# Mixer B of a two-layer decoder trunk: group weights made in token rows and sent through scratch memory

## The chip, the cores and the metric

The kernel runs on one core of one Trainium2 chip. The metric is the device time of one execution in microseconds, as the median of several runs; lower is better. The trace is that of one profiled execution, and its times count from the start of its span.

## The reference

A trunk of two layers over 1024 tokens of width 1024, all in float32. Layer 1 is causal attention with a forget gate and a gated convolutional feed-forward network. Layer 2 begins with mixer B, which the change is in: three groups g = 0, 1, 2 of 8 heads each (head width 64), group g attending over tokens that lie 1, 4 or 16 apart. Every group gives, for each token and head, an output o_g and the logarithm of its softmax denominator, and the three are merged:

```
m = jnp.max(s, axis=-1, keepdims=True)
p = jnp.exp(s - m)
l = jnp.sum(p, axis=-1, keepdims=True)
o = einsum("bnrhij,bnjrhd->bnirhd", p / l, vv)
lse = (m + jnp.log(l))[..., 0]
...
alpha = jax.nn.softmax(jnp.stack(lses, axis=0), axis=0)
o = jnp.sum(alpha[..., None] * jnp.stack(outs, axis=0), axis=0)
x = x + o.reshape(B, S, B_OUT_WIDTH) @ b_w_out[bl]
```

After it come a second feed-forward network and a last norm.

## The kernel before

Activations lie with the features on the 128 partitions and the tokens along the free axis. Every float32 product of the projections is made as three matmuls of split halves (`mm3`, L114 to L116, 512 columns each).

Mixer B runs over 12 units (p, g): p counts four pairs of heads (j = 0, 1), and for each p the groups come in the order 2, 1, 0. `attend_b` (L488) works on one unit in two halves m of the tokens. `scores_b` (L459) makes the scores of one block of 128 queries (L475, L476) with the block's tokens on the partitions; for g = 1 and 2 the order of tokens is by residue, so that a block holds tokens that lie 4 or 16 apart. `softmax` (L251) adds the bias and takes the negative maximum `nm` on VectorE (L254), the exponential and its sum `ls` on ScalarE (L259), the reciprocal of the sum on VectorE (L261), and multiplies the probabilities by it on GpSimd (L262). `transposed_pv` turns the probabilities (L232, `tp`), splits them into `pt` (L150 on ScalarE, L151 on VectorE), and multiplies with the values into `po` (L245). `add_parts` adds the two halves of `po` into the group's output `og` (a ScalarE copy into `otmp`, L267, and a VectorE addition, L268).

When all three groups of a pair are there, `each_half` (L1281) takes the logarithm of all sums (L1273), subtracts the maxima (L1274), and calls `merge_b` (L520) for each half of 512 tokens. `merge_b` copies the statistics so that each value stands 64 times side by side (`lx`, L535), and turns them with TensorE so that each token's value lies on the 64 partitions of its head: four transposes for g = 0 (L539), four for g = 1 (L541), and eight matmuls against parts of the identity for g = 2 (L544; the trace counts two instructions for each, so 16 per half). Then maxima, differences, exponentials, sums, reciprocals and weighted additions run over tiles of 128x512 on VectorE, ScalarE and GpSimd (L548 to L564). The result is split by `emit_o` (L570) and written to scratch memory `o_sp` (for the last pair: kept in `yh`, `yl`).

Beside the attention, `weave` takes instructions from a filler: the projections of the unit ahead (`tasks_b`, L1217; their weights come by `load_half`, L82: one DMA on SyncE's queue into `wraw`, a gain on GpSimd at L89, a cast into `wh` at L92, a difference into `wl` at L93). In the last unit (3, 0) the filler is the first half of the output projection (`out_proj`, L600), which starts when the first token half of the last pair is merged. Earlier results come back from `o_sp` and the residual from `x_sp` at the start of that unit (`reload`, L582). The order of the instructions on each engine is set when the kernel is built, by a scheduler that simulates the engines and moves instructions against the order of the program; on the chip each engine and each DMA-issuing queue runs its list in that order.

Of the kernel before, what the change touches and what calls it, by code (L numbers as in the profile page):

```python
# [8 lines left out]
F32 = mybir.dt.float32  # L9
# [41 lines left out]
def trunk(ctx, tc, x, a_w_in, a_b_f, a_w_out, b_w_q, b_w_out, kv_norm_g, w_kv,  # L51
# [23 lines left out]
    aug = dram.tile([A_HEADS, 2, 4, S], F32, name="aug")  # L75

# [174 lines left out]
    def softmax(t, sc_cuts, masks, nm, l, rl):  # L251

        for ci, ((sc, a, b), m) in enumerate(zip(sc_cuts, masks)):
            nc.vector.tensor_tensor_reduce(  # L254
                out=t[:, a:b], in0=sc, in1=m, scale=1.0,
                scalar=INIT if ci == 0 else nm[ci - 1], op0=ALU.add, op1=ALU.min,
                accum_out=nm[ci])
# [3 lines left out]
        nc.vector.reciprocal(rl, l)  # L261
        nc.gpsimd.tensor_scalar(out=t[:, :n], in0=t[:, :n], scalar1=rl, scalar2=1.0,  # L262
                                op0=ALU.mult, op1=ALU.mult)

    def add_parts(dst, po, tmp, view=lambda t: t):

        nc.scalar.copy(tmp, po[64:P])  # L267
        nc.vector.tensor_tensor(out=dst, in0=view(po[0:64]), in1=view(tmp), op=ALU.add)  # L268
# [95 lines left out]
    def attend_a(ap, ps_, u, heads, v, last):  # L364
        psc, ptr, pov = ps_

        def values(qg, j, probs, o):
# [10 lines left out]
            tmp = ap.tile([P, 2 * P], F32, name="otmp", bufs=1)  # L378
            add_parts(o[js], po[:, :2 * P], tmp[js])
# [79 lines left out]
    def scores_b(ap, psc, p, g, j, head, nm, ls, m):  # L459
# [6 lines left out]
        rl = ap.tile([P, 4], F32, name="rl", bufs=2)  # L466
        cell = {}
        for b in range(4 * m, 4 * m + 4):
# [12 lines left out]
                    [nm[:, g, j, b:b + 1]], ls[:, g, j, b:b + 1],  # L481
                    rl[:, b - 4 * m:b - 4 * m + 1])
# [5 lines left out]
    def attend_b(ap, ps_, p, g, heads, v, og, nm, ls, each_half):  # L488
        psc, ptr, pov = ps_

        def values(m, j, cell):
# [14 lines left out]
            tmp = ap.tile([P, H2], F32, name="otmp", bufs=1)  # L506
            add_parts(in_order(g, og[js], m), po, tmp[js], residues(g))
# [4 lines left out]
        for m in range(2):  # L512
            for j in range(2):
                cell = yield from scores_b(ap, psc, p, g, j, heads[j], nm, ls, m)
# [5 lines left out]
    def merge_b(ap, psc, ls, os, hf):  # L520

        sl = half(hf)
        lt = []
        for g in range(NG):

            tp = psc.tile([P, H2], F32, name="sc")
            tpr = tp.rearrange("p (t r) -> p r t", r=DILS[g])
            blocks = [4 * hf + i for i in range(4)] if g == 0 else (
                [2 * i + hf for i in range(4)] if g == 1 else list(range(NB)))
            for i, b in enumerate(blocks):  # L530
                if i % 4 == 0:
                    lx = ap.tile([P, 4, 2, 64], F32, name="lx", bufs=2)
                    step = 2 if g == 1 else 1
                    src = ls[:, g, :, b:b + 4 * step - step + 1:step]
                    nc.scalar.copy(lx, src.rearrange("p j b -> p b j").unsqueeze(3)  # L535
                                   .to_broadcast([P, 4, 2, 64]))
                lb = lx[:, i % 4].rearrange("p j d -> p (j d)")
                if g == 0:
                    nc.tensor.transpose(tp[:, i * P:(i + 1) * P], lb, ident)  # L539
                elif g == 1:  # L540
                    nc.tensor.transpose(tpr[:, i], lb, ident)  # L541
                else:
                    own = ident.rearrange("p (r t) -> p r t", r=2)[:, :, 32 * hf:32 * hf + 32]
                    nc.tensor.matmul(tpr[:, 2 * b:2 * b + 2], lb, own, start=True, stop=True)  # L544
            lt.append(tp)
        mx = ap.tile([P, 4, 2, 64], F32, name="lx", bufs=2).rearrange("p b j d -> p (b j d)")
        e = [ap.tile([P, H2], F32, name=f"e{g}") for g in range(NG)]
        nc.scalar.copy(mx, lt[0])  # L548
        for g in (1, 2):
            nc.vector.tensor_tensor(out=mx, in0=lt[g], in1=mx, op=ALU.max)  # L550
        for g in range(NG):
            nc.vector.tensor_tensor(out=e[g], in0=lt[g], in1=mx, op=ALU.subtract)
            nc.scalar.activation(e[g], e[g], AF.Exp)
        nc.gpsimd.tensor_tensor(out=mx, in0=e[0], in1=e[1], op=ALU.add)
        nc.gpsimd.tensor_tensor(out=mx, in0=mx, in1=e[2], op=ALU.add)
        for i in range(4):
            c = slice(i * P, (i + 1) * P)
            nc.vector.reciprocal(mx[:, c], mx[:, c])  # L558
        for g in range(NG):
            eng = nc.gpsimd if g < 2 else nc.vector  # L560
            eng.tensor_tensor(out=e[g], in0=os[g][:, sl], in1=e[g], op=ALU.mult)
        nc.vector.tensor_tensor(out=e[1], in0=e[1], in1=e[2], op=ALU.add)
        nc.vector.tensor_tensor(out=e[0], in0=e[0], in1=e[1], op=ALU.add)
        nc.vector.tensor_tensor(out=e[0], in0=e[0], in1=mx, op=ALU.mult)  # L564
        return e[0]
# [624 lines left out]
    with ExitStack() as st:  # L1190
# [71 lines left out]

        filler = stream([t for i in range(len(units)) for t in tasks_b(i)])
# [70 lines left out]
```

## Time and profile before

| | us |
|---|---|
| median of 3 runs (2672.45 to 2673.91) | 2672.62 |
| the profiled execution | 2673.07 |
| its span, first to last instruction | 2671.2 |
| mixer B after its first projections, up to its last unit | about 1380 to 1880 |
| mixer B's last unit, up to the first matmul of the output projection | 1880 to 1919 |
| output projection, both halves | 1919 to 1965 |

In the views, PE is TensorE's matmuls, PEld its weight loads, DVE VectorE, ACT ScalarE, POOL GpSimd, SP SyncE. "Busy" is the time in which an engine had an instruction running; matmuls overlap, so the mean duration of one is longer than the time by which the next follows it. In a row of groups the numbers behind the bar are busy us, mean ns of one, and the idle time of the engine just before them with what ended it.

### The profile page before, as it was taken

How to read it: one execution, taken by the hardware profiler on the slowest of the kernel's cores; microseconds unless marked ns; L12 is line 12 of the kernel's file. 1: busy time of each engine (PE TensorE's matmuls, PEld its weight loads, DVE VectorE, ACT ScalarE, POOL GpSimd, SP SyncE). 2: the span in 40 equal slices, each digit the busy share in tenths (PEclk: the TensorE clock that was granted, in tenths of full speed). 3: DMA queues.
4: the chain of work that ended last, by engine and by line, in shares of the span. 5: the costliest groups of instructions: out<-in, count | busy, mean ns of one | idle time of the engine just before them, and what ended most of it. 6: DMA issues, size and time to landing. Idle time of an engine off the chain costs nothing.

```text
span 2671.2 us, 37824 instructions
## 1 busy us (share of the span) xinstructions
PE 2590.0 (97%) x12913; PEld 2165.8 (81%) x12913; DVE 2000.6 (75%) x4037; ACT 1378.6 (52%) x2893; POOL 658.0 (25%) x841
## 2 busy tenths in 40 slices
PE   7999999999999999999899999999889999999998
PEld 5898888787788888888688888888667888888887
DVE  6676777777877777778867777777798677776787
ACT  6566666654534444444545656665645434444444
POOL 0222322310122112112223453534301111111121
PEclk8999999999999999999999999999899999999999
DMA  5121211522111111111411111112321111111113
GB/s 183 51 64 50 57 50 56 195 87 91 44 52 49 54 52 58 53 52 47 145 36 36 45 43 40 41 36 76 115 91 48 48 56 48 53 59 56 48 48 114
DMA packets 251241, 175.40 MB, mean 66 GB/s; under 512 B 12448, under 2 KB 231208, under 8 KB 251048
## 3 DMA queue, kind: packets, MB, share of 16 engines
q1 hardware_dynamic: 250936, 172.96, 21.3%
q8 instruction: 102, 1.67, 0.3%
q14 instruction: 91, 0.75, 0.1%
q10 hardware_dynamic: 112, 0.02, 0.0%
HBM read 145.06 MB, written 23.68 MB: 63 GB/s over the span
## 4 chain that ended last, share of the span: by engine, by line
PE 85%; DVE 8%; ACT 3%; issue 2%; DMA 2%; POOL 0%; POOLq 0%; SPq 0%; ACTq 0%; DVEq 0%
PE up L754 30%; PE mm L114 13%; PE mm L115 13%; PE mm L116 13%; PE po L245 4%; PE tp L232 3%; PE sc L353 1%; DVE u L705 1%; PE sc L354 1%; DVE lx L558 1%; PE up L114 1%; DVE t L254 1%; PE sc L476 1%; PE sc L475 1%; PE up L115 1%
## 5 line engine op out<-in xcount | busy, mean ns | idle before, releaser
L114 PE MATMUL mm<-yh,wh 128*128 128x512 f32 x960 | 381.3, 398 | 12.2 <-ACT yh L150 5.9
L115 PE MATMUL mm<-yl,wh 128*128 128x512 f32 x960 | 379.5, 395 | 1.2 <-DMA yl<-o_sp 1.2
L116 PE MATMUL mm<-yh,wl 128*128 128x512 f32 x960 | 379.6, 395 | 0.0
L150 ACT CAST wh<-wraw 128x512 fp32r<-128x512 f32 x228 | 140.9, 619 | 353.8 <-PE up L754 306.7
L859 DVE TENSOR_TENSOR xT<-mm,xT 128x512 f32<-128x512 f32 x320 | 217.9, 684 | 108.8 <-PE mm L116 107.0
L151 DVE TENSOR_TENSOR wl<-wraw,wh 128x512 fp32r<-128x512 f32 x228 | 165.9, 733 | 152.1 <-ACT wh L150 152.0
L754 PE MATMUL up<-yh,wh 128*128 128x512 f32 x704 | 274.4, 390 | 0.9 <-ACT wh L150 0.9
L754 PE MATMUL up<-yl,wh 128*128 128x512 f32 x704 | 274.1, 389 | 0.0
L754 PE MATMUL up<-yh,wl 128*128 128x512 f32 x704 | 268.9, 389 | 0.0
L259 ACT ACTIVATE t<-t,nm 128x128 f32<-128x128 f32 (+4 forms) x320 | 185.2, 580 | 86.2 <-DVE nm L254 84.0
L115 PE MATMUL mm<-ml,wh 128*128 128x512 f32 x576 | 225.3, 391 | 1.4 <-DVE ml L151 1.4
L114 PE MATMUL mm<-mh,wh 128*128 128x512 f32 x576 | 224.8, 390 | 0.0
L116 PE MATMUL mm<-mh,wl 128*128 128x512 f32 x576 | 223.9, 389 | 0.0
L114 PEld LDWEIGHTS mm<-yh,wh 128*128 128x128 f32 x960 | 181.1, 189 | 49.8 <-ACT yh L150 6.2
L116 PEld LDWEIGHTS mm<-yh,wl 128*128 128x128 f32 x960 | 181.0, 188 | 34.3
L115 PEld LDWEIGHTS mm<-yl,wh 128*128 128x128 f32 x960 | 181.3, 189 | 33.8 <-DMA yl<-o_sp 1.4
L738 POOL TENSOR_TENSOR sraw<-fraw 128x512 f32<-128x512 f32 x40 | 67.1, 1677 | 547.3 <-DMA fraw<-in_ffn_w_up_dram 385.6
L150 ACT CAST pt<-tp 128x128 fp32r<-128x128 f32 (+2 forms) x408 | 148.6, 381 | 96.3 <-PE tp L232 55.2
L151 DVE TENSOR_TENSOR pt<-tp,pt 128x128 fp32r<-128x128 f32 (+2 forms) x408 | 168.7, 430 | 34.5 <-ACT pt L150 32.1
L245 PE MATMUL po<-pt,v 128*128 128x256 f32 x1040 | 190.0, 292 | 2.4 <-ACT pt L150 1.0
L245 PEld LDWEIGHTS po<-pt,v 128*128 128x128 f32 x1040 | 154.5, 191 | 17.3 <-DVE pt L151 1.5
L93 DVE TENSOR_TENSOR wl<-wraw,wh 128x512 fp32r<-128x512 f32 x176 | 129.4, 738 | 50.7 <-ACT wh L92 43.0
(350 smaller groups left out, 6307.6 us busy)
## 6 DMA issues: line engine op xcount, KB each, us to landing
wraw<-in_ffn_w_down_dram SPq DMA_DIRECT2D x104, 256.0 KB
fraw<-in_ffn_w_up_dram SPq DMA_DIRECT2D x88, 256.0 KB
wraw<-in_ffn_w_up_dram SPq DMA_DIRECT2D x88, 256.0 KB
wraw<-in_a_w_in_dram SPq DMA_DIRECT2D x60, 256.0 KB
wraw<-in_w_kv_dram SPq DMA_DIRECT2D x48, 256.0 KB
wraw<-in_a_w_out_dram SPq DMA_DIRECT2D x32, 256.0 KB
xT<-x_sp SPq DMA_DIRECT2D x32, 256.0 KB
wraw<-in_b_w_q_dram SPq DMA_DIRECT2D x24, 256.0 KB
```

The costliest lines, as they stand in the source:

```text
L93: nc.vector.tensor_tensor(out=wl, in0=raw, in1=wh.bitcast(F32), op=ALU.subtract)
L114: nc.tensor.matmul(ps, ah, bh, start=(i == 0), stop=False)
L115: nc.tensor.matmul(ps, ah, bl, start=False, stop=False)
L116: nc.tensor.matmul(ps, al, bh, start=False, stop=(i == n - 1))
L150: nc.scalar.copy(h, src)
L151: return nc.vector.tensor_tensor(out=l, in0=src, in1=h.bitcast(F32), op=ALU.subtract).ins
L232: nc.tensor.transpose(tp[:, i * P:(i + 1) * P], c, ident)
L245: nc.tensor.matmul(po[:, col:col + 2 * P], v(kb), pt[:, hl, i * 2 * P:(i + 1) * 2 * P], start=(first and i == 0 and hl == 0), stop=(last a ...
L259: nc.scalar.activation(t[:, :n], t[:, :n], AF.Exp, bias=nm[len(sc_cuts) - 1], scale=-1.0, accum_out=l)
L738: nc.gpsimd.tensor_tensor(out=raw[n], in0=raw[a], in1=raw[b], op=op)
L754: nc.tensor.matmul(ps[bank], a[:, c], b[:, k], start=(start and k == 0 and i == 0), stop=(k == KH - 1 and i == 2), skip_group_check=True)
L859: nc.vector.tensor_tensor(out=xT[:, d, sl], in0=ps, in1=xT[:, d, sl], op=ALU.add)
```

## The change

Probabilities stay unnormalised in mixer B: `softmax` gets no `rl` there, and its reciprocal (L261) and GpSimd multiplication (L262) are left out (layer 1 keeps them). The negative maxima and the sums of a pair are kept in one tile `st`, 32 columns for each group. When a unit is done, `spread` turns its 32 columns with one transpose into 32 rows of 128 tokens, copies them to SBUF, and writes them to scratch memory in the order of the tokens. `group_weights` reads them back for one token half as rows of 32 tokens on 32 partitions, makes the three weights exp(max difference) / (weighted sum) there, writes them to scratch, and reads them repeated on 64 partitions for each head. `merge_b` then is three multiplications and two additions. For the first three pairs, the weights are made in the middle of the next pair's first unit and the merge runs at its end; for the last pair both follow at once, half by half. `add_parts` writes the ScalarE copy straight to its destination and adds onto it, without `otmp`.

```
-        nc.vector.reciprocal(rl, l)
-        nc.gpsimd.tensor_scalar(out=t[:, :n], in0=t[:, :n], scalar1=rl, ...)
+        if rl is not None:   # the same two, for layer 1 alone
...
+    def add_parts(dst, po):
+        nc.scalar.copy(dst, po[0:64])
+        nc.vector.tensor_tensor(out=dst, in0=po[64:P], in1=dst, op=ALU.add)
...
+    def spread(ap, psc, st, g, dst, ms=(0, 1)):
+        n = 16 * len(ms)
+        tp = psc.tile([P, H2], F32, name="sc")
+        nc.tensor.transpose(tp[:n, :P], st[:, g, 16 * ms[0]:16 * ms[0] + n], ident)
+        rows = ap.tile([32, P], F32, name="srow")
+        if g < 2:
+            nc.scalar.copy(rows[:n], tp[:n, :P])
+        else:
+            nc.scalar.copy(rows.rearrange("n (m l h) -> n m l h", m=2, h=2),
+                           tp[:n, :P].rearrange("n (h m l) -> n m l h", h=2, m=2))
+        if g == 0:
+            for i, m in enumerate(ms):
+                nc.sync.dma_start(dst[0, m].rearrange("k j (b t) -> (k j b) t", t=P),
+                                  rows[16 * i:16 * i + 16])
+        elif g == 1:
+            v = dst[1].rearrange("m k j (t r) -> r (m k j) t", r=4)
+            for r in range(4):
+                nc.sync.dma_start(v[r], rows[8 * r:8 * r + 8])
+        else:
+            for k in range(2):
+                for j in range(2):
+                    i = 16 * k + 8 * j
+                    for m in range(2):
+                        nc.sync.dma_start(
+                            dst[2, m, k, j].rearrange("(l b h) -> b l h", b=8, h=2),
+                            rows[i:i + 8, 64 * m:64 * m + 64].rearrange("b (l h) -> b l h", h=2))
+
+    def group_weights(ap, src, dst, m):
+        T = 32
+        r = ap.tile([32, NG, 2, T], F32, name="stats")
+        for k in range(2):
+            nc.sync.dma_start(r[:, :, k], src[:, m, k].rearrange("g j (b t) -> (j b) g t", t=T))
+        mn, sm = (ap.tile([32, T], F32, name=n) for n in ("mn", "sm"))
+        e = ap.tile([32, NG, T], F32, name="ew")
+        el = r[:, :, 1]
+        nc.vector.tensor_tensor(out=mn, in0=r[:, 0, 0], in1=r[:, 1, 0], op=ALU.min)
+        nc.vector.tensor_tensor(out=mn, in0=mn, in1=r[:, 2, 0], op=ALU.min)
+        for g in range(NG):
+            nc.vector.tensor_tensor(out=e[:, g], in0=r[:, g, 0], in1=mn, op=ALU.subtract)
+        nc.scalar.activation(e, e, AF.Exp, scale=-1.0)
+        nc.vector.tensor_tensor(out=el, in0=e, in1=el, op=ALU.mult)
+        nc.vector.tensor_tensor(out=sm, in0=el[:, 0], in1=el[:, 1], op=ALU.add)
+        nc.vector.tensor_tensor(out=sm, in0=sm, in1=el[:, 2], op=ALU.add)
+        nc.vector.reciprocal(sm, sm)
+        for g in range(NG):
+            nc.vector.tensor_tensor(out=e[:, g], in0=e[:, g], in1=sm, op=ALU.mult)
+        nc.sync.dma_start(dst[m].rearrange("g j (b t) -> (j b) g t", t=T), e)
+        w = ap.tile([P, NG, H2], F32, name="wb", bufs=2)
+        for j in range(2):
+            nc.sync.dma_start(w[64 * j:64 * j + 64],
+                              dst[m][:, j].unsqueeze(0).to_broadcast([64, NG, H2]))
+        return w
+
+    def merge_b(os, w, m, eng):
+        o = [t[:, half(m)] for t in os]
+        for g in (2, 1, 0):
+            (eng if g else nc.vector).tensor_tensor(out=o[g], in0=o[g], in1=w[:, g], op=ALU.mult)
+        nc.vector.tensor_tensor(out=o[1], in0=o[1], in1=o[2], op=ALU.add)
+        nc.vector.tensor_tensor(out=o[0], in0=o[0], in1=o[1], op=ALU.add)
+        return o[0]
...
             def each_half(m):
+                if last:
+                    spread(ap, psc, st, 0, stat_sp[p], (m,))
+                    out_half(p, ogs, group_weights(ap, stat_sp[p], wt_sp[p], m), m, nc.vector)
+                    return
+                if due:
+                    pp, os, ws = due[0]
+                    if m == 0:
+                        ws += [group_weights(ap, stat_sp[pp], wt_sp[pp], hf) for hf in range(2)]
+                    else:
+                        for hf in range(2):
+                            out_half(pp, os, ws[hf], hf, nc.gpsimd)
+                        due.clear()
+                if m == 1:
+                    spread(ap, psc, st, g, stat_sp[p])
+                    if g == 0:
+                        due.append((p, ogs, []))
```

## Rows read from the trace of the kernel before

**Rows 1.** The page's first part: busy time, share of the span and instructions.
```profile
PE 2590.0 (97%) x12913; PEld 2165.8 (81%) x12913; DVE 2000.6 (75%) x4037; ACT 1378.6 (52%) x2893; POOL 658.0 (25%) x841
```

**Rows 2.** Windows: length; busy (count) of PE, PEld, DVE, ACT, POOL; clock, DMA share, GB/s.
```profile
1380.00:1880.00 500.00, 495.76 (x2737) 426.58 (x2735) 377.00 (x1038) 302.99 (x826) 222.25 (x381) 1.00 0.17 50
1880.00:1919.00 39.00, 28.02 (x152) 23.04 (x152) 31.01 (x94) 29.27 (x76) 15.84 (x29) 0.80 0.26 91
1919.00:1965.00 46.00, 43.66 (x200) 34.76 (x199) 39.08 (x64) 25.14 (x46) 5.74 (x4) 0.98 0.39 114
```

**Rows 3.** Groups by line on PE, 1380 to 1880 us: merge_b's turns.
```profile
L544 PE MATMUL sc<-ident,lx 128*128 128x64 f32 x96 | 12.2, 267 | 0.0
...
L539 PE MATMUL sc<-ident,lx 128*128 128x128 f32 x24 | 3.6, 272 | 0.0
```

**Rows 4.** Timeline of PE in the first merge: start us, us, instruction.
```profile
1497.28 0.60 PE L539 MATMUL sc<-ident,lx 128*128 128x128 f32 x4
1497.72 0.60 PE L541 MATMUL sc<-ident,lx 128*128 128x128 f32 x4
```

**Rows 5.** Groups by line on DVE, 1380 to 1880 us.
```profile
L268 DVE TENSOR_TENSOR og<-po,otmp 64x512 f32<-64x512 f32 x42 | 40.1, 955 | 8.3 <-ACT otmp L267 7.5
...
L261 DVE RECIPROCAL rl<-ls 128x1 f32<-128x1 f32 x176 | 25.9, 157 | 18.9 <-ACT t L259 16.8 <-POOL t L262 0.4
L558 DVE RECIPROCAL lx<-lx 128x128 f32<-128x128 f32 x24 | 20.3, 909 | 3.0 <-POOL lx L555 3.0
...
L552 DVE TENSOR_TENSOR e<-sc,lx 128x512 f32<-128x512 f32 x18 | 11.5, 682 | 0.2
```

**Rows 6.** Groups by line on ACT, 1380 to 1880 us.
```profile
L535 ACT COPY lx<-ls 128x512 f32<-128x512 f32 x24 | 14.4, 619 | 2.9 <-PE sc L541 1.0 <-PE sc L544 0.7 <-PE sc L539 0.6
...
L553 ACT ACTIVATE e<-e 128x512 f32<-128x512 f32 x18 | 10.5, 628 | 3.1 <-DVE e L552 3.1
L1273 ACT ACT_TABLE_LOAD x4 | 5.1, 1283 | 0.1
```

**Rows 7.** Groups by line on POOL, 1380 to 1880 us.
```profile
L262 POOL TENSOR_SCALAR t<-t,rl 128x128 f32<-128x128 f32 (+1 forms) x176 | 80.8, 467 | 94.5 <-DVE rl L261 73.7 <-PE tp L232 5.0 <-PE sc L476 4.3
...
L561 POOL TENSOR_TENSOR e<-og,e 128x512 f32<-128x512 f32 x12 | 16.1, 1363 | 0.0
```

**Rows 8.** Timeline of mixer B's last unit, all engines.
```profile
1889.01 0.19 ACT L259 ACTIVATION_READ_ACCUMULATOR t<-t,nm 128x1 f32 x1
...
1906.40 0.68 DVE L268 TENSOR_TENSOR og<-po,otmp 64x512 f32<-64x512 f32 x1
...
1908.79 3.38 DVE L558 RECIPROCAL lx<-lx 128x128 f32<-128x128 f32 x4
...
1917.70 0.76 DVE L151 TENSOR_TENSOR yl<-e,yh 128x256 fp32r<-128x256 f32 x2 [0.27 <-ACT yh L150]
...
1919.04 1.05 PE L114 MATMUL mm<-yh,wh 128*128 128x512 f32 x2
```

**Rows 9.** Timeline: small operations on DVE and ACT.
```profile
1890.66 0.21 ACT L1273 ACTIVATE ls<-ls 128x8 f32<-128x8 f32 x1
...
1983.40 0.16 DVE L160 TENSOR_TENSOR nt<-nt,nms 128x4 f32<-128x4 f32 x1
```

**Rows 10.** The chain that ended last, in order of time: start us, us, what.
```profile
1525.10 1.69 DMA o_sp<-ol
...
1943.15 4.90 DMA wraw<-in_ffn_w_up_dram
```

**Rows 11.** Timeline of a load of 1024 pieces of 64 bytes, and its first use.
```profile
3.00 0.38 SPq L1067 DMA_DIRECT2D graw<-in_a_w_in_dram  x1
...
9.11 0.30 ACT L150 CAST wg<-graw 128x128 fp32r<-128x128 f32 x1 [0.53 <-DMA graw<-in_a_w_in_dram]
```

**Rows 12.** Waits, 1370 to 1950 us: who waited for whom, us in total, times, longest.
```profile
ACT wh L92 <- PE mm L115: 46.7, 35, 3.2
```

**Rows 13.** Waits of SyncE's queue, 1380 to 1950 us.
```profile
SPq L87 <- DVE wl L93: 378.5, 55, 36.1
```

More of the change, by code (lines that the diff above doesn't have):

```diff
@@ L75, in trunk @@
     aug = dram.tile([A_HEADS, 2, 4, S], F32, name="aug")
+    stat_sp = [dram.tile([NG, 2, 2, 2, H2], F32, name=f"stat{p}") for p in range(HPG // 2)]
+    wt_sp = [dram.tile([2, NG, 2, H2], F32, name=f"wt{p}") for p in range(HPG // 2)]
     yh = yp.tile([P, KD, S], F32R, name="yh")
@@ L260, in softmax @@
                              scale=-1.0, accum_out=l)
-        nc.vector.reciprocal(rl, l)
[L262 to L268, printed above, removed]
+        if rl is not None:
+            nc.vector.reciprocal(rl, l)
+            nc.gpsimd.tensor_scalar(out=t[:, :n], in0=t[:, :n], scalar1=rl, scalar2=1.0,
+                                    op0=ALU.mult, op1=ALU.mult)
+    def add_parts(dst, po):
+        nc.scalar.copy(dst, po[0:64])
+        nc.vector.tensor_tensor(out=dst, in0=po[64:P], in1=dst, op=ALU.add)
     w_in = a_w_in[0]
@@ L377, in values @@
             js = slice(64 * j, 64 * j + 64)
-            tmp = ap.tile([P, 2 * P], F32, name="otmp", bufs=1)
-            add_parts(o[js], po[:, :2 * P], tmp[js])
+            add_parts(o[js], po[:, :2 * P])
             if j:
@@ L480, in scores_b @@
                     [bias[:, :P] if g == 2 else bias[:, 2 * P - n:]],
-                    [nm[:, g, j, b:b + 1]], ls[:, g, j, b:b + 1],
-                    rl[:, b - 4 * m:b - 4 * m + 1])
+                    [stat(st, g, 0, j, b)], stat(st, g, 1, j, b), None)
             for kb in range(lo, b + 1):
@@ L505, in values @@
                                          (bi == 0, bi == len(banks) - 1), groups)
-            tmp = ap.tile([P, H2], F32, name="otmp", bufs=1)
-            add_parts(in_order(g, og[js], m), po, tmp[js], residues(g))
+            add_parts(in_order(g, og[js], m), residues(g)(po))
             if j:
@@ L513, in attend_b @@
             for j in range(2):
-                cell = yield from scores_b(ap, psc, p, g, j, heads[j], nm, ls, m)
+                cell = yield from scores_b(ap, psc, p, g, j, heads[j], st, m)
                 if waiting:
@@ L518, in attend_b @@
         yield from values(*waiting)
-    def merge_b(ap, psc, ls, os, hf):
-        sl = half(hf)
-        lt = []
-        for g in range(NG):
[L526 to L550, printed above, removed]
-        for g in range(NG):
[L552 to L565, printed above, removed]
@@ new lines, in stat @@
+    def stat(st, g, k, j, b):
+        c = (16 * (b // 4) + 8 * k + 4 * j + b % 4, 4 * b + 2 * k + j, 16 * k + 8 * j + b)[g]
+        return st[:, g, c:c + 1]
+    def spread(ap, psc, st, g, dst, ms=(0, 1)):
[24 more added lines that the diff above has]
+                            rows[i:i + 8, 64 * m:64 * m + 64].rearrange("b (l h) -> b l h", h=2))
@@ L1268, in trunk, with out_half @@
             if g == 2:
[L1269 to L1277 removed]
+                st = ap.tile([P, NG, 32], F32, name="st", bufs=2)
+                ogs = [None] * NG
+            ogs[g] = ap.tile([P, S], F32, name=f"og{g}", bufs=1 + (g == 2))
+            def out_half(pp, os, w, m, eng):
+                o = merge_b(os, w, m, eng)
                 for c in range(2):
[L1279 removed]
+                    emit_o(ap, pp, 2 * m + c, o[:, c * 2 * P:(c + 1) * 2 * P], last)
             def each_half(m):
[L1282 to L1290 removed]
+                if last:
[4 more added lines that the diff above has]
+                    pp, os, ws = due[0]
+                    if m == 0:
+                        ws += [group_weights(ap, stat_sp[pp], wt_sp[pp], hf) for hf in range(2)]
[7 more added lines that the diff above has]
+                        due.append((p, ogs, []))
             if last:
```

24 lines of the change are left out of this document (4 added, 20 removed).

## Prediction

> **What bounds the kernel now.** I read the page's first part first: TensorE is busy for 97% of the span, no other engine above 75% [rows 1]. Then I cut mixer B into windows. From 1380 to 1880 us PE is busy for 495.76 of 500 us with the granted clock at 1.00, that is at the higher level of 2.4 GHz all along, while VectorE stands at 75%, ScalarE at 61% and GpSimd at 44% [rows 2]. So in this stretch the time is the sum of what PE issues, and the other engines' waits are covered by projection matmuls; of stalls there are only 4.24 us to win. The last unit is another regime: from 1880 to 1919 PE has 28.02 us of work in 39 us at a clock of 0.80 (a part at 1.2 GHz, after idle stretches), and VectorE and ScalarE are busy for 80% and 75% [rows 2]. There no projections are left to fill, and the output projection waits for the first merged half. From 1919 to 1965 PE is busy again for 43.66 of 46 us. The change has to be priced in these two regimes apart: PE's instructions in the first, the length of a chain in the second.
>
> **What goes from PE in the bulk (1380 to 1880).** Three of the four pairs are merged here, six halves, with 24 L539, 24 L541 and 96 L544 instructions, 144 in all [rows 3], where L541 repeats L539. A group's mean of some 0.27 us holds latency that overlaps; the step from one to the next is the price. Four L539 begin at 1497.28 and the L541 behind them at 1497.72 [rows 4], 0.11 us each. 144 x 0.11 = 15.8 us. The change adds one transpose for each of the 11 units that end here, 11 x 0.11 = 1.2 us. Net 14.6 us. Bounds: the groups' busy time is 12.2 + 3.6 and about 3.6 again for L541 = 19.4 us, an upper end, as it counts the tail of each group; if a quarter of these small matmuls hid beside others, 12 less 1.2, or 10.8 us. I take 14.6, since PE has no gaps in which anything could hide.
>
> **What goes from the other engines there.** VectorE loses 176 reciprocals (25.9 us), 24 large ones (20.3 us) and the merge's tiles of 128x512, of which L552 alone is 11.5 us for 18 [rows 5]: the maxima, two products and two sums are 36 more of that kind at 0.68 us, 24.5 us. That is 82 us. It gets, for each of six halves, 12 small operations at 0.16 us [rows 9] and one product and two sums at 0.68 us, 4.0 us or 24 us in all. ScalarE loses the copies L535 (14.4 us), the exponentials L553 (10.5 us), and table loads of 1.28 us each [rows 6], since no logarithm is taken any more, and gets a copy per unit and a small exponential per half (0.21 us [rows 9]). GpSimd loses 80.8 us of L262, and its two products per half (1.36 us each) stay [rows 7]. All of this costs and gives nothing directly: it lies beside PE, which is 99% busy. It does shorten the way from scores to `pt` by one VectorE and one GpSimd step for every block, so I count 2 of the 4.24 us of stalls as won (0 to 4). `add_parts` now reads its addend with the stride it writes with; L268 already takes 955 ns in the mean [rows 5], and even half of that again on 42 of them, 20 us, stays below what VectorE was freed of. Nothing on this engine is late next.
>
> **DMAs, and who stands behind them.** Each of the first three pairs adds 8 + 4 + 2 writes of statistics and, per half, two reads, one write and two repeated reads: 24 DMAs, all on SyncE's queue, with 0.38 us of issue each as for the load of rows 11: 9 us per pair. Behind them in that queue stand the weight loads L87 and the writes of `o_sp`. The queue has room: its L87 sat 378.5 us waiting for a buffer [rows 13], so loads run as far ahead as the buffers let them, and the casts L92 wait for PE to free `wh` rather than for data [rows 12]. Six `wh` tiles hold three tasks of two tiles; 33 tasks in 500 us are 15 us each, so the cover is one to two tasks, 15 to 30 us. The weights are asked for in the middle of a unit of 45 us and used at its end, which is longer than the chain worked out below, so I cost this at nothing (0 to 15 us per pair; see the rivals). The merge reads `og0` and `og1`, which have one buffer each, before the next unit writes them; the next unit's first scores lie between. Nothing.
>
> **The tail (1880 to 1965).** Before, the first half's statistics are ready at 1889.2, its last group's output at 1907.1; then come exponentials, additions, the 3.38 us of reciprocals, products, and the split until 1918.5; the projection starts at 1919.04 [rows 8]. After, the chain from the statistics is: a transpose and a copy 0.7; write, read, write, and repeated read, four trips of a DMA; 12 small VectorE operations and an exponential, 12 x 0.16 + 0.21 = 2.1 bare [rows 9], taken as 4 among other work in order on VectorE; merge 5 x 0.68 and a split of 0.9, 4.3. For a trip, the nearest rows are the write of a split that frees its buffer after 1.69 us and a weight load used 4.90 us after its issue, with two more behind it [rows 10]. The first three are small, 2.2 us each; the last is two transfers of 384 KB, 4 us: 10.6 us, with ends at 6.8 and 19.6. So 1889.2 + 0.7 + 10.6 + 4 + 4.3 = 1908.8, between 1903 and 1918. But the output itself bounds it too: 1907.1 less what the lighter ScalarE and VectorE give, say 1904, plus a merge of 4.3 is 1908. Ten us are to be had at the start, yet not all at the end, because what the second half of the attention leaves to do on PE then moves behind the start of the projection. At the end of the tail 48 more small turns go, 5.3 us by the step above, of PE work that was partly idle time. I take 6 us for the tail: bounds a loss of 6 (every trip at the higher end, and VectorE held while it waits) and a gain of 14 (PE's idle time in the first two tail windows, 10.98 and 2.34 us [rows 2], nearly all won).
>
> **Sum.** 14.6 + 2 + 6 = 22.6; less a microsecond of stalls that the new order will bring somewhere, 21.6. The profiled execution took 2673.07 us with a span of 2671.2, so 2651.5; it lies 0.45 us above the median shown, which gives 2651.
>
> **Rivals.**
> *The tail's chain is late.* If the trips take the higher end and wait behind weight loads of the projection in SyncE's queue, the projection starts at 1925, 6 us later than before: the tail loses 6 instead of giving 6, and the time is 2663. For it: four trips in series where none stood; eight weight loads of `b_w_out` stand on the same queue in just that stretch. Against it: most of the chain runs beside the rest of the attention.
> *SyncE's queue is held.* Each half makes the queue stand still for two landings and a VectorE stretch: 2 x 4.9 + 5, some 15 us, 30 for both halves; with a cover of 15 to 30 us PE could be left without weights for up to 15 us a pair. At 7 us a pair the gain is gone: 2651 + 21 = 2672. Against it: the scheduler places a waiting DMA when its simulation has it ready, and loads run ahead [rows 12, 13].
> *A flood of single elements makes it slower.* The writes of g = 1 go to every fourth token: 4 DMAs of 1024 elements of 4 bytes each per unit, and g = 2 writes pairs, 2048 pieces. The load of 1024 pieces of 64 bytes was used 6.1 us after its issue, behind others [rows 11]; taken as the price that is 24.4 us for g = 1, and 49 if half the transfer engines do the work. All later transfers stand behind it. It decides where it exceeds the cover by over 5.4 us in each of four units, from about 27 us on; at 49 us against a cover of 30 the loss is 4 x 19 = 76 us, and the time 2727. Against it: 6.1 us holds a whole trip and the wait behind the input's loads, so it is an upper end; the share of the DMA engines in the bulk is 0.17 [rows 2]. The Trainium skill warns of exactly this, in "DMA: Bandwidth & Descriptors", section "Rules for kernel authors": a strided last dimension becomes one descriptor per element. The same page, in "Why a DMA increments its semaphore by 16 and not by 1", would put the 8 rows of such a write on 8 of the 16 engines. No row of this trace shows either.
>
> **How the numbers follow.** Forecast 0.62; tail late 0.14; queue held 0.12; flood 0.07; other reorderings 0.05. What counts as no change is within 0.2%, 5.3 us. Faster by more: 0.62 + 0.14 and part of the queue's case, 0.79; the same: most of the queue's case, 0.09; slower: 0.12. The range goes from 2638 (upper ends of the bulk, 18.2 + 4, and of the tail, 14, less a little) up to 2669, which takes in a late tail and half a held queue.
>
> **What would show it.** Right: L539 to L544 gone and PE's count in the bulk lower by some 130, its busy share there still 99%, the bulk shorter by 15 to 17 us, the projection's first matmul some 10 us earlier after the start of the last unit. Wrong: idle time on PE before L114 that ends on `wh` or `wl`; long waits of SyncE's queue on `wt` or `stat`; VectorE idle before the new `mn` or the merge's products, with `pt` late behind it.

## The result, and the profile after

The changed kernel takes 2688.45 us (median of 4 runs, 2685.90 to 2691.35) against 2673.26 us before (4 runs, 2672.45 to 2674.16): a ratio of 1.0057 with a 95% interval of 1.0040 to 1.0074. It is slower by some 15 us; forecast were 2651 us, and the range ended at 2669. The prediction was wrong.

The profiled execution took 2687.51 us, with a span of 2685.7 us. First the busy times of its page, to be held against [rows 1]:

```profile
PE 2576.5 (96%) x12734; PEld 2148.6 (80%) x12734; DVE 1953.0 (73%) x3859; ACT 1334.9 (50%) x2832; POOL 546.7 (20%) x629
```

Every engine does less than before: PE by 13.5 us, VectorE by 48, ScalarE by 44, GpSimd by 111. What the change was to remove is gone, and the span is longer all the same by 14.5 us. So the time went into waiting. To see where, I cut at marks that every version has: the first scores of mixer B, the first scores of its last unit, the first matmul of the output projection, and the end. Before, these lie at 1377.5, 1879.3, 1919.0 and 2671.2 us; after, at 1376.1, 1882.4, 1928.5 and 2685.7. The bulk has become 4.5 us longer (501.8 to 506.3), the last unit 6.4 (39.7 to 46.1), and what follows 5.0 (752.2 to 757.2). These are the windows after (length, then busy time and count of PE, PEld, DVE, ACT and POOL, then granted clock, DMA share, GB/s), with the bulk before ahead of them; the last five are stretches of the bulk after, and its three merges lie in the second, the fourth and the fifth:

```profile
1377.50:1879.30 501.80, 497.56 (x2747) 428.14 (x2745) 378.13 (x1045) 304.73 (x827) 222.25 (x381) 1.00 0.17 49
```
```profile
1376.10:1882.40 506.30, 491.81 (x2627) 418.19 (x2625) 333.27 (x882) 282.62 (x792) 125.37 (x195) 0.99 0.29 58
1882.40:1928.50 46.10, 22.48 (x118) 18.04 (x117) 25.69 (x86) 17.99 (x59) 2.62 (x8) 0.72 0.58 126
...
1376.10:1500.00 123.90, 123.90 (x673) 106.47 (x672) 75.45 (x202) 73.24 (x202) 29.24 (x48) 1.00 0.24 36
1500.00:1545.00 45.00, 39.02 (x204) 32.75 (x203) 35.03 (x98) 22.11 (x69) 15.44 (x20) 0.96 0.33 89
1545.00:1640.00 95.00, 95.00 (x515) 81.67 (x514) 59.70 (x149) 54.95 (x148) 21.94 (x37) 1.00 0.26 38
1640.00:1690.00 50.00, 45.87 (x238) 38.37 (x237) 37.36 (x107) 24.63 (x77) 16.90 (x22) 0.97 0.34 86
...
1785.00:1830.00 45.00, 40.63 (x207) 32.32 (x206) 33.10 (x90) 22.15 (x72) 16.86 (x22) 1.00 0.32 89
```

Between the merges PE is busy without a gap. At each merge it stands still: 5.98 us in the first, 4.13 in the second, 4.37 in the third. That is all of the bulk's 14.5 us of idle time, against 4.2 before. The clock dips to 0.96 and 0.97 at the first two. The change's own new step is where the bulk loses. The reader sees why in the first merge, on VectorE (start, duration, instruction, in brackets the idle time before it and what ended it):

```profile
1528.34 1.80 DVE L589 TENSOR_TENSOR og<-og,wb 128x512 f32<-128x512 f32 x1 [3.60 <-DMA wb<-wt]
1530.07 0.28 DVE L153 TENSOR_TENSOR pt<-tp,pt 128x128 fp32r<-128x128 f32 x1
1531.30 1.52 DVE L590 TENSOR_TENSOR og<-og,og 128x512 f32<-128x512 f32 x1 [0.96 <-POOL og L589]
```

L589 is VectorE's product of the second token half (that of the first half stands at 1511.94). VectorE runs its list in order; the product waits 3.60 us for the repeated weights (`wb`) to land, and behind it stands the `pt` that PE needs. PE's row of the same moment, with SyncE's issues of the weights:

```profile
1530.40 0.58 PE L247 MATMUL po<-pt,v 128*128 128x256 f32 x1 [3.80 <-DVE pt L153]
```
```profile
1518.93 0.46 SPq L578 DMA_DIRECT2D wt<-ew  x1
...
1521.59 1.24 SPq L581 DMA_DIRECT2D wb<-wt  x2
```

The weights are written at 1518.93, asked back at 1521.59 and used at 1528.34, 6.75 us later, by a product that the scheduler put there. In the program the weights are made in the middle of this unit and merged at its end; the unit's first scores begin at 1507.68 and the next unit's at 1561.08. The rows of waits over the bulk (who waited for whom, us in total, times, longest) show it for all three merges, VectorE once in each:

```profile
POOL og L589 <- DMA wb<-wt: 21.7, 6, 3.8
...
DVE og L589 <- DMA wb<-wt: 10.4, 3, 3.7
```

SyncE's queue, which two rivals had in view, is not what holds the bulk: its wait for a weight buffer, 378.5 us before [rows 13], still has 179.4 us of room, and none of PE's longer idle times in the bulk ends on a weight:

```profile
SPq L89 <- DVE wl L95: 179.4, 42, 12.9
```

The last unit loses in another way. The rows of SyncE, ScalarE, VectorE and PE there, which answer to [rows 8]:

```profile
1875.86 10.90 SPq L548 DMA_DIRECT2D stat<-srow  x4
1886.86 4.20 SPq L614 DMA_DIRECT2D yh<-o_sp  x1
...
1896.22 7.66 SPq L617 DMA_DIRECT2D xT<-x_sp  x8
1904.22 1.04 SPq L89 DMA_DIRECT2D wraw<-in_b_w_out_dram  x2
1905.59 0.34 SPq L543 DMA_DIRECT2D stat<-srow  x1
```
```profile
1897.04 0.25 ACT L537 COPY srow<-sc 16x128 f32<-16x128 f32 x1 [1.88 <-DMA stat<-srow]
1910.45 0.25 ACT L537 COPY srow<-sc 16x128 f32<-16x128 f32 x1 [9.32 <-DMA stat<-srow]
```
```profile
1911.96 0.18 DVE L567 TENSOR_TENSOR mn<-stats 32x32 f32<-32x32 f32 x1 [12.02 <-DMA stats<-stat]
```
```profile
1913.43 0.90 PE L234 MATMUL tp<-ident,t 128*128 128x128 f32 x3 [11.60 <-DVE pt L153]
```

L548 is the write of group 1's statistics, four DMAs of 1024 single elements each. Their issue alone holds SyncE's queue for 10.90 us, the reload of earlier results (L614 to L617) comes after it, and the write of group 0's statistics (L543) only at 1905.59. The single buffer `srow` is still being read by the former DMA at each copy of ScalarE. VectorE stands for 12.02 us before the first `mn`, PE for 11.60, and the clock is 0.72 in the stretch.

### The profile page after: what moved, and what is told of

It reads as the page before. It is cut to its first block, busy times and chain, and to the rows that moved or that the text cites. A ratio compares the mean times of both kernels' runs of the same rounds, so it can differ in the third digit from the quotient of the medians.

```text
span 2685.7 us, 36967 instructions
## 1 busy us (share of the span) xinstructions
PE 2576.5 (96%) x12734; PEld 2148.6 (80%) x12734; DVE 1953.0 (73%) x3859; ACT 1334.9 (50%) x2832; POOL 546.7 (20%) x629
## 4 chain that ended last, share of the span: by engine, by line
PE 82%; DVE 9%; DMA 4%; ACT 3%; issue 2%; POOL 0%; SPq 0%; POOLq 0%; ACTq 0%; DVEq 0%
PE up L781 29%; PE mm L116 13%; PE mm L117 13%; PE mm L118 13%; PE po L247 4%; PE tp L234 3%; DVE u L732 1%; DVE t L257 1%; PE sc L357 1%; DMA wb<-wt 1%; PE sc L358 1%; PE up L116 1%; PE up L118 1%; PE up L117 1%; DVE pt L153 1%
## 5 line engine op out<-in xcount | busy, mean ns | idle before, releaser
L247 PE MATMUL po<-pt,v 128*128 128x256 f32 x1040 | 195.6, 294 | 19.8 <-DVE pt L153 14.7
L781 PEld LDWEIGHTS up<-yh,wh 128*128 128x128 f32 x704 | 132.2, 188 | 29.8 <-ACT wh L152 1.8
```

The costliest lines, as they stand in the source:

```text
L247: nc.tensor.matmul(po[:, col:col + 2 * P], v(kb), pt[:, hl, i * 2 * P:(i + 1) * 2 * P], start=(first and i == 0 and hl == 0), stop=(last a ...
L781: nc.tensor.matmul(ps[bank], a[:, c], b[:, k], start=(start and k == 0 and i == 0), stop=(k == KH - 1 and i == 2), skip_group_check=True)
```

## The experiments

Each kernel differs from the changed one by what its diff shows. The table has what all of them gave (bulk: first scores to the last unit's first scores; last unit: to the output projection's first matmul; rest: to the end; all from one profiled execution, us). Each ratio is to runs of the kernel before that were made along with that kernel; the medians of these lie between 2670.77 and 2673.26, so differences of medians between rows are good to some 2 us.

| kernel | median (range) | ratio to before, 95% | bulk | last unit | rest |
|---|---|---|---|---|---|
| before | 2673.26 (2672.45 to 2674.16) | | 501.8 | 39.7 | 752.2 |
| changed | 2688.45 (2685.90 to 2691.35) | 1.0057 [1.0040, 1.0074] | 506.3 | 46.1 | 757.2 |
| e1_rows | 2674.33 (2672.48 to 2675.60) | 1.0009 [1.0000, 1.0019] | 504.6 | 32.4 | 757.7 |
| e2_const_w | 2647.54 (2645.75 to 2648.63) | 0.9910 [0.9895, 0.9924] | 484.1 | 30.4 | 750.7 |
| e3_no_stats | 2635.03 (2632.90 to 2635.73) | 0.9862 [0.9847, 0.9877] | 481.8 | 21.4 | 751.0 |
| e4_unscaled | 2677.87 (2674.59 to 2680.95) | 1.0020 [1.0011, 1.0029] | 506.0 | 38.7 | 750.8 |
| p1_pinned | 2699.39 (2696.29 to 2699.69) | 1.0100 [1.0085, 1.0115] | 518.5 | 45.8 | 754.0 |
| f1_g1_rows | 2675.37 (2673.57 to 2679.02) | 1.0014 [1.0004, 1.0023] | 503.5 | 32.7 | 756.4 |
| f2_both | 2686.22 (2685.56 to 2688.98) | 1.0056 [1.0041, 1.0071] | 518.2 | 33.4 | 756.8 |
| f3_tail | 2685.24 (2681.98 to 2685.95) | 1.0048 [1.0033, 1.0063] | 516.1 | 33.4 | 754.2 |
| m1_merge_pin | 2657.43 (2655.87 to 2658.44) | 0.9948 [0.9933, 0.9963] | 488.7 | 33.4 | 756.4 |
| m2_merge_tail | 2654.85 (2650.41 to 2657.71) | 0.9937 [0.9923, 0.9952] | 489.3 | 32.1 | 753.4 |
| q1_rows_pins | 2659.54 (2656.37 to 2660.78) | 0.9958 [0.9941, 0.9975] | 490.8 | 32.2 | 754.6 |
| m0_merge_only | 2669.20 (2663.60 to 2671.27) | 0.9989 [0.9979, 0.9998] | 488.5 | 45.3 | 754.5 |

**e1_rows.** Are the small pieces the cost, and where?

```
-            v = dst[1].rearrange("m k j (t r) -> r (m k j) t", r=4)
+            v = dst[1].rearrange("m k j (r t) -> r (m k j) t", r=4)
...
-                            dst[2, m, k, j].rearrange("(l b h) -> b l h", b=8, h=2),
+                            dst[2, m, k, j].rearrange("(b x) -> b x", b=8),
```

> The changed kernel, but the statistics of groups 1 and 2 are written as runs of 512 and 256 bytes instead of single elements and pairs (so the statistics of these groups land in the order of the residues, not of the tokens); same number of DMAs, same bytes, same waits. Theory 'single elements' (the write queue and the transfer engines are clogged by 4-byte and 8-byte pieces, and everything behind them is late, the weights of the merge too): the time falls from 2688 to about 2655, the stalls of TensorE at the three merges and the 12 us of VectorE before the last pair's weights go. Theory 'landing' (VectorE stands in order before trips of a DMA that land later than the order of instructions was made for, whatever the size of their pieces): the tail gains some 10 us, since the single row buffer of the statistics comes free in time, and the three merges keep their 8 us of stalls each: about 2677.

It is 14 us faster than the changed kernel, and nearly all of that lies in the last unit (46.1 to 32.4); the bulk stays at 504.6. That is what the theory of the landing had (about 2677, with the stalls kept). So the small pieces cost the tail, and hardly anything in the bulk.

**e2_const_w and e3_no_stats.** What is left when the wait, and then the statistics too, are gone?

```
     def group_weights(ap, src, dst, m):
+        return w_const[0]        # a tile filled with 0.5
```
```
-                    spread(ap, psc, st, g, stat_sp[p])   # e3: neither of the two spreads
```

> The changed kernel, but the merge multiplies by a constant tile; the weights are not made, read or written (the statistics are still turned and written to scratch). Theory 'landing': no instruction of VectorE or GpSimd waits for a DMA at the merges any more, so the bulk takes about 487 us from the first scores to the last unit's instead of 506, and in the tail only the row buffer's wait stays: about 2655. Theory 'single elements': the queue is as full as before, weight loads and the reload come as late as in the changed kernel, and the time stays above 2672.

> As the constant-tile kernel, and the statistics are not turned or written either: what is left of the change is unscaled probabilities, the addition of the two halves in place, and a merge of three products and two sums with a constant tile. Both theories: the bulk is some 15 us shorter than in the kernel before (about 487 us) and the tail some 8 us shorter; about 2648. If it is not below 2655, the forecast was also wrong about what TensorE gains by the turns left out.

The bulk of e2, then of e3:

```profile
1379.90:1864.00 484.10, 483.78 (x2628) 415.50 (x2626) 325.81 (x812) 280.05 (x786) 126.21 (x195) 1.00 0.26 50
```
```profile
1376.80:1858.60 481.80, 481.80 (x2624) 416.19 (x2622) 328.21 (x815) 280.68 (x776) 128.31 (x195) 1.00 0.18 54
```

With weights that are simply there, PE has almost no gap and the bulk is 17.7 us shorter than before, with the merge's products, sums and the transposes all in it: PE's busy time is 13.8 us lower and its idle time 3.9. The gain that the forecast counted is real; it is the weights' way that takes it back, 22.2 us in the bulk. The spread adds 2.3 us in the bulk and 9.0 in the last unit. Both kernels came out faster than expected, by 7 and 13 us, the larger part of it behind the bulk.

**e4_unscaled.** The kernel before, with only the scaling of the probabilities left out: does that one part gain?

```
-        nc.vector.reciprocal(rl, l)
-        nc.gpsimd.tensor_scalar(out=t[:, :n], in0=t[:, :n], scalar1=rl, ...)
+        if rl is not None:   # the same two; None in mixer B
```

> The kernel before with one part of the change alone: the reciprocal and the GpSimd product of every block of mixer B are left out (the output of a group is then not normalised); the merge is the old one. Both theories, and the forecast: nothing in the bulk, where TensorE is busy all along, and 2 to 5 us in the tail, where the path from scores to the turned probabilities loses two steps: 2668 to 2673.

It is slower by some 5 us, though 176 instructions on each of two engines are gone in the bulk. The order came out anew, and VectorE's reciprocals of the old merge now stand ahead of an operation that PE waits for:

```profile
1535.77 3.39 DVE L557 RECIPROCAL lx<-lx 128x128 f32<-128x128 f32 x4 [0.47 <-POOL lx L554]
...
1539.82 0.69 DVE L443 SCALAR_TENSOR_TENSOR s<-mm,s 64x512 fp32r<-64x512 f32 x1
```
```profile
1540.66 0.47 PE L114 MATMUL mm<-yh,wh 128*128 128x512 f32 x1 [2.36 <-DVE s L443]
```

Such stalls (2.36, 2.11 and 1.43 us at the three merges) are 5.9 us, while PE's idle time in the bulk as a whole rose by 3.2 us (4.2 to 7.4) and the bulk by 4.2. They may be most of it, but no run takes them away, so it stays argued. The last unit and the rest are 2.4 us shorter together, as expected. Work taken off engines with room brought nothing in the bulk here.

**p1_pinned.** The theory that VectorE stands too early before a landing: move weights and merges of the first three pairs late. `issue_after` adds an order on one engine, no wait.

```
+                        with tc.issue_after(pin["dve"]):     # last addition of the unit's middle
                             ws += [group_weights(...) for hf in range(2)]
...
+                        with tc.issue_after(pin["dve"]), tc.issue_after(pin["pool"]):
                             for hf in range(2):
                                 out_half(pp, os, ws[hf], hf, nc.gpsimd)
```

> The changed kernel with its computation untouched; only the order of instructions is held: for the first three pairs the small operations that make the weights are queued on VectorE behind the addition of the first token half of the unit they are written in, and the merge's products and sums behind the addition of its second half (on GpSimd behind the last bias), so that the DMAs have landed long before. Theory 'landing': the three stretches of stalled TensorE in the bulk go, first scores to the last unit's first scores in about 486 us instead of 506, the tail as in the changed kernel: about 2668. Theory 'single elements' alone: the pieces are as many and lie where they lay; no gain beyond 5 us, above 2683.

A clear miss: 11 us slower than the changed kernel. The bulk went to 518.5 us.

**f1_g1_rows, f2_both, f3_tail.** f1 writes group 1's statistics in the order of the tokens, as e1 did not, and still in rows: four transposes with strided destinations, each followed by a copy of 8 rows and one DMA of 8 rows of 512 bytes. f2 is f1 and p1 together; f3 also queues the merge of the last half behind the split of the half before.

```
+        if g == 1:
+            tpr = tp[:8].rearrange("n (t r) -> n r t", r=4)
+            for r in range(4):
+                nc.tensor.transpose(tpr[:, r], st[:, 1, 8 * r:8 * r + 8], ident)
+            for c in range(4):
+                row = rows[32 * c:32 * c + 8]
+                nc.scalar.copy(row, tp[:8, c * P:(c + 1) * P])
+                nc.sync.dma_start(flat[:, c * P:(c + 1) * P], row)
```

> The changed kernel with the statistics of group 1 put in the order of the tokens by four small transposes into every fourth column, and written as rows of 512 bytes; group 2 still writes pairs of elements; the order of the merge is not held. If the clog comes from group 1's single elements, the tail is that of the kernel with runs for both groups, about 2675; the bulk keeps its stalls. If group 2's pairs do it, the time stays near 2688.

> Both of these: group 1's statistics as rows, and the order of weights and merges held for the first three pairs. The two theories add: about 2688 - 14 - 20 = 2654, which would beat the kernel before by 0.7%.

> As the kernel with both, and in the last unit the merge of the second token half is queued on VectorE behind the split of the first, so that the first half's split does not stand behind a landing of the second half's weights. The projection's wait of 3.4 us on that split should go, and some of the 5 us between the projection's start and the feed-forward network: about 2650.

f1 gives what e1 gave, 13 us, again in the last unit. So of the small pieces it is group 1's single elements. f2 and f3 missed by over 30 us, as their bulk has p1's trouble. It shows in f2's first merge:

```profile
1543.98 6.74 SPq L561 DMA_DIRECT2D stat<-srow  x5
...
1551.31 0.45 SPq L585 DMA_DIRECT2D wt<-ew  x1
1558.64 1.24 SPq L588 DMA_DIRECT2D wb<-wt  x2
```
```profile
1565.09 0.69 DVE L596 TENSOR_TENSOR og<-og,wb 128x512 f32<-128x512 f32 x1 [8.06 <-DMA wb<-wt]
```
```profile
1570.05 0.58 PE L479 MATMUL sc<-m,s 128*128 128x256 f32 x1 [10.54 <-DVE st L257]
```

Asked for late, the weights come to stand in SyncE's queue behind group 2's writes (L561, pieces of 8 bytes), their own write lands only 7 us after its issue, and VectorE waits 8.06 us in one piece. I had moved the request as late as its use. The theory of the landing was not refuted by this, but neither was it shown.

**m1_merge_pin, m2_merge_tail, q1_rows_pins.** Now the merge alone is moved and the weights are left early (m1, with f1's writes); m2 adds f3's tail. q1 keeps everything late, as p1, but has e1's writes in runs.

```
-                        with tc.issue_after(pin["dve"]):      # p1; not in m1
                             ws += [group_weights(...) for hf in range(2)]
...
                         with tc.issue_after(pin["dve"]), tc.issue_after(pin["pool"]):
                             for hf in range(2):
                                 out_half(pp, os, ws[hf], hf, nc.gpsimd)
```

> The changed kernel with group 1's statistics written as whole rows of 512 bytes, and with the merges of the first three pairs alone queued behind VectorE's last addition and GpSimd's bias of the middle of the next unit; the weights (group_weights) are left where the scheduler puts them, early. Theory, engines in order that wait for a landing: the repeated rows have landed long before the merge comes, so the three stalls of TensorE at the merges go (some 20 us less than with group 1's rows alone): about 2655, first scores to last unit's first scores 485 to 490 us. Rival, the merge's own work: its products and sums (some 7 us of VectorE in one piece) hold VectorE for two halves whether or not anything has landed, and TensorE stalls as often: about 2675. Rival of the pinned kernels, the trips themselves: a wait for the small landing inside the weights' chain remains, a stall of some 4 us per pair: about 2665.

> The kernel with merges queued late (m1_merge_pin) and, in the tail, the last half's merge queued behind the split of the half before. If the landing of the second half's weights delays the first half's split (2.9 us of waiting seen in the changed kernel), it gains 2 to 4 us on m1_merge_pin; if the tail is bound by the chain of its four trips, nothing.

> The changed kernel with weights and merges queued late as in p1_pinned, and the statistics of groups 1 and 2 both written in runs of 512 and 256 bytes (the tokens come out in the wrong order). Theory: the pinned kernels failed because the weights' DMAs, asked for late, stand in SyncE's queue behind group 2's 2048 pieces of 8 bytes of the same unit (6.7 us of issue). Then without those pieces the stalls at the merges are gone or half as long: 2655 to 2662. Rival, the chain of trips in itself is too long to be asked for late (weights pinned, VectorE waits for wb in any case): stalls of 7 to 10 us per pair remain: 2670 to 2680.

m1 came where the theory put it: 2657.43 us. Its second weights are asked back at 1518.08; VectorE's products begin at 1559.32:

```profile
1518.08 1.23 SPq L588 DMA_DIRECT2D wb<-wt  x2
```
```profile
1558.20 1.10 DVE L272 TENSOR_TENSOR og<-po,og 64x512 f32<-64x512 f32 x1
1559.32 0.69 DVE L596 TENSOR_TENSOR og<-og,wb 128x512 f32<-128x512 f32 x1
```
```profile
1545.00:1590.00 45.00, 45.00 (x240) 38.00 (x239) 32.34 (x78) 26.10 (x71) 10.48 (x17) 1.00 0.24 59
```

No bracket stands behind the product, no wait for `wb` is left in the bulk's rows, and PE is busy for 45.00 of 45 us around VectorE's part of the merge. The work of the merge is the same, so the rival by which it keeps the three stalls has fallen. What is left of it is one wait at the first merge: GpSimd's four products stand together at 1527.04 (5.05 us), and a `pt` that GpSimd fills is late behind them:

```profile
1533.61 0.62 PE L247 MATMUL po<-pt,v 128*128 128x256 f32 x3 [1.76 <-POOL pt L241]
```

q1 says why the late weights failed: with the pieces in runs the same late order gives a bulk of 490.8 us, in place of 518.5 in p1 and of 518.2 in f2, which has group 2's pieces alone. The rows of q1's first merge, to be held against those of f2, show the five writes of group 2 issued in 1.84 us in place of 6.74, and the weights asked back 2.4 us after they are written in place of 7.3:

```profile
1544.01 1.84 SPq L556 DMA_DIRECT2D stat<-srow  x5
...
1547.15 0.31 SPq L580 DMA_DIRECT2D wt<-ew  x1
1549.59 1.24 SPq L583 DMA_DIRECT2D wb<-wt  x2
```

m2's gain on m1 is 2.6 us in the medians, as expected, but their ranges overlap; its last unit and rest are shorter by 4.3 us in the profiled executions.

**m0_merge_only.** The changed kernel with m1's move alone, group 1's single elements left in.

```
+                        with tc.issue_after(pin["dve"]), tc.issue_after(pin["pool"]):
                             for hf in range(2):
                                 out_half(pp, os, ws[hf], hf, nc.gpsimd)
```

> The changed kernel with one thing altered: the merges of the first three pairs queued behind VectorE's last addition and GpSimd's bias of the middle of the next unit, as in m1_merge_pin; group 1's single elements stay. If the two causes are independent (stalls at the merges in the bulk, single elements in the tail), the stretch from mixer B's first scores to the last unit's is 488 to 491 us as in m1_merge_pin (506.3 in the changed kernel), the tail is as long as in the changed kernel, and the time is 2670 to 2674, no different from before. Rival: the single elements also delay the landings in the bulk, so the merges stall still: 2680 to 2688. Rival: the tail too recovers, since SyncE's queue is less held when the merges come later: about 2657.

The bulk is 488.5 as in m1, and the last unit 45.3, as in the changed kernel. Moving the merge alone gives 19.3 us (2688.45 to 2669.20), rows in place of elements alone 13.1 (to 2675.37), both 31.0 (to 2657.43), against a sum of 32.4. The two causes add up, as far as the runs can tell.

## Why the prediction was wrong

**PE's share of the bulk: right.** 14.6 us for the turns and 2 for stalls, less 1, make a bulk of 486.2 us. e2 has 484.1, with 13.8 us for PE's work and 3.9 for stalls, and the kernels with late merges have 488.5 to 489.3.

**The step that failed: the DMAs and who stands behind them.** "The weights are asked for in the middle of a unit of 45 us and used at its end, which is longer than the chain" was read from the program. On the chip the scheduler moved both forward: in the first merge the repeated rows are asked for at 1504.79 and 1521.59, the first time before the unit's first scores (1507.68), and the second half's product stands 6.75 us after its request, in the first half of the unit. VectorE, which has other engines' work behind it, waits there in order. That the scheduler's simulation had the landing at this place is likely, but no trace shows the simulation. What was costed at nothing costs 17.8 us over three merges: 506.3 against 488.5 in m0, where only the place of the merge is held differently:

```profile
1379.70:1868.20 488.50, 485.80 (x2627) 416.50 (x2626) 329.62 (x882) 282.85 (x791) 124.92 (x195) 1.00 0.29 60
```

Of these, 11.8 us are PE's idle time and 6.0 are longer busy time for as many instructions, with the clock at 0.99 in place of 1.00. That alone exceeds the 14.6. My sentence "nothing on this engine is late next" looked at VectorE's sum of work and not at what one waiting instruction does to its queue. The last part of the prediction named the sign, VectorE idle before the merge's products with `pt` late behind it, but no rival had it with a price.

**The flood of single elements: right in kind, wrong in place and size.** It was rated 0.07, put into the bulk, and priced at 76 us against the cover of the weight loads. In the bulk that cover held (e1's and f1's bulk is shorter by only 1.7 and 2.8 us). With the weights asked for late it did not hold: there group 2's pairs cost some 27 us of bulk (q1 against f2 and p1). In the changed kernel it struck in the one unit without cover: 13 to 14 us by e1 and f1, and the last unit and the rest lost 11.4 us where they were forecast to win 6. The sum had failed here too: it took 0.38 us for the issue of each DMA, and one of 1024 elements took 1.48 in the median and up to 5.30. That each element makes a piece of its own is shown by the page's count of packets under 512 bytes, of the changed kernel and of f1:

```profile
DMA packets 282467, 182.12 MB, mean 68 GB/s; under 512 B 40480, under 2 KB 259368, under 8 KB 282280
```
```profile
DMA packets 266213, 182.14 MB, mean 68 GB/s; under 512 B 24097, under 2 KB 243113, under 8 KB 266025
```

The difference is 16383, and group 1 writes 16 DMAs of 1024 elements, 16384. The Trainium skill, "DMA: Bandwidth & Descriptors", section "Rules for kernel authors", states just this (a strided last dimension becomes one descriptor per element), and the trace agrees.

Where the 13 us lie is seen by holding the rows of f1 against those of the changed kernel, as their last units begin at 1882.6 and 1882.4:

```profile
1895.53 0.33 SPq L550 DMA_DIRECT2D stat<-srow  x1
1896.89 0.81 SPq L568 DMA_DIRECT2D stats<-stat  x2
```

The first copy into `srow` begins at 1895.25 in f1 and 1.8 us later in the changed kernel (1897.04), which is its wait for that buffer. From the copy to the issue of its write 8.6 us go by in place of 0.3 (1905.59): the queue is still at the reload that stands behind group 1's writes, and at two weight loads. From the write to its reading back 4.8 us go by in place of 1.4 (1910.39).

**The tail's chain: its length right, its gain only in part.** From the first half's statistics to the projection the forecast had 19.6 us. Measured from the copy of these statistics, f1 has 20.1, m2 19.7 and the changed kernel 31.5. The four trips come to 10.6 us in m2, as forecast, but as 1.4, 1.6, 1.4 and 6.2 and not as three of 2.2 and one of 4, so there the sum was lucky. The gain is another matter. In f1 the projection starts 32.7 us after the last unit's first scores, 7.0 us sooner than before, but 4.2 of these are given back in the rest: net 2.8, and 2.1 in m1. q1 has 5.1, and m2, which also queues the second half's merge later, has 6.4 against the 6 forecast. The rival of a late chain got its size, 6.4 us later after the last unit's first scores for the 6 it named, and the queue in which the chain stands; but what stood ahead there was group 1's writes and the reload, not above all the projection's weights.

**SyncE's queue held: not in the bulk.** No run shows PE waiting there for weights of the projections. In the last unit the queue was held, as above.

**The account.** Forecast was a span of 2649.6 us, measured 2685.7. Of the 36.1 us the bulk has 20.1 (506.3 against 486.2), the last unit and the rest 17.4 (803.3 against 785.9), and mixer B begins 1.4 us earlier. m2, with both causes mended, has 489.3 and 785.5, a span of 2651.9 us, and a median of 2654.85: faster than both kernels, by 0.6% than before. It still lacks 5.2 us of bulk that e2 has: 2.4 are PE's wait at the first merge for the `pt` behind GpSimd's products, as in m1; the other 2.8 are mostly busy time, and weren't looked into.

## What to carry to other kernels

A result that comes back through memory should be asked for early and its first reader queued late, past the landing, on every engine that runs in order: the order that counts is that of the engine's list in the trace, not of the program. The Trainium skill gives this rule in "DMA: Bandwidth & Descriptors", section "Rules for kernel authors" (issue early, compute, wait late); m0 and p1 show both halves of it, since moving the request along with the reader lost 11 us where moving the reader alone won 19. In q1, where no small pieces fill the queue, the late request cost hardly anything against m1 (2659.54 and 2657.43 us, with ranges that overlap). Price a step's DMAs by their pieces, and look for the stretch in which nothing covers them.

## What the runs showed of the hardware

Issuing a DMA of 1024 single elements can take SyncE far longer than one of 8 rows of 512 bytes. The rows of these writes in the changed kernel and in f1 (durations in ns: least, median, longest; first and last start):

```profile
L548 SPq DMA_DIRECT2D stat<-srow x16: 732/1484/5300, 1449.4 to 1881.5; - x16
```
```profile
L542 SPq DMA_DIRECT2D stat<-srow x16: 263/278/302, 1452.2 to 1878.7; - x16
```

The merge's product of 128x512 on VectorE took 0.69 us in m1, where none ran beside it at 1559.32. Beside GpSimd's products of the same shape it went, in these rows, by which engine began first. At 1528.34 in the changed kernel, 0.01 us behind GpSimd, VectorE's took 1.80 us. At 1565.09 in f2 and at 1669.18 in the changed kernel, 0.04 and 0.01 us ahead of GpSimd, it took 0.69, and at the latter GpSimd's first product took 1.81 us, in place of 1.29 where it ran alone in m0. GpSimd's rows of the first two places, of the changed kernel and of f2 (two products each):

```profile
1528.33 2.94 POOL L589 TENSOR_TENSOR og<-og,wb 128x512 f32<-128x512 f32 x2 [3.61 <-DMA wb<-wt]
```
```profile
1565.13 2.99 POOL L596 TENSOR_TENSOR og<-og,wb 128x512 f32<-128x512 f32 x2 [5.25 <-DMA wb<-wt]
```
